# Prologue of a two-batch encoder layer: loads moved to a second queue, the first token tile done one weight tile at a time

## The chip, the cores and the metric

One NeuronCore of a Trainium2 chip runs the whole program. The metric is the device time of one execution in microseconds, the median of the runs shown. The engines are named as the profile names them: PE (TensorE), PEld (its weight loads), DVE (VectorE), ACT (ScalarE), POOL (GpSimd), SP (SyncE, which here only issues transfers).

## The reference, cut to what matters

One encoder layer with shared weights is applied to 512 sample tokens and 256 prompt tokens of width 1024, all float32:

```python
def _mixer(xn, w_in, ...):
    proj = xn @ w_in                       # (S, 1024) @ (1024, 4096)
    aq, ak, av, hq, hf_f, hf_b, hi, hg = jnp.split(proj, offs, axis=-1)
    ...
def _encode(x, norm_mix_pre, w_in, ...):
    mix = _mixer(_rmsnorm(x, norm_mix_pre[l]), w_in[l], ...)
    x = x + _rmsnorm(mix, norm_mix_post[l])
    ffn = _conv_ffn(_rmsnorm(x, norm_ffn_pre[l]), ...)
    x = x + _rmsnorm(ffn, norm_ffn_post[l])
```

The case is about the first step: the normalisation of x before the mixer, and the first block of columns of `xn @ w_in`, the 512 columns of `hi` (the values of the recurrent heads).

## The kernel before, in words

The 768 tokens are six tiles of 128 rows, x0 to x5. The weights come as a list of tiles of 1024 x 128 (512 KB each); the first four, W0 to W3, are the columns of `hi`, and W4 and on belong to the gates that follow. A weight tile lands in one of three RAW buffers (`raw`, line 209). `split` (line 231) turns it into a rounded high part (ACT, line 242) and a low part, tile minus high part (DVE, line 243), and then issues the load of the tile three further on (line 238), into the buffer that the DVE instruction has just read: that load waits on SP for that DVE instruction.

A token tile passes through `prenorm_rows` (line 307): half of its square sum on ACT (line 311), half on DVE (line 312), the mean (DVE, line 314), a power on POOL (line 304), then the scaling, two DVE instructions of 512 columns (line 317). `prenorm_transpose` (line 320) makes eight PE transposes into two PSUM banks, and `prenorm_evac` (line 326) splits them into a high part (two ACT copies, line 808) and a low part (two DVE subtractions, line 809).

`value_tile(n, i, ...)` (line 341) multiplies token tile i with weight tiles n and n+1: for each of eight k three products, high x high, low x high, high x low, 24 matmuls of 256 columns (line 346). The second of them already needs the low part of the tokens.

`run` (line 1099) writes this in program order: tile 0, W0, W1, tile 1, W2 and W3, then a loop over the tiles with `value_tile(0, i)`, transposes and evacuation of tile i+1, `prenorm_rows(i + 2)`, `value_tile(2, i)`. On SP and POOL the instructions stand in that program order (`manual_schedule`, line 1349). On PE, ACT and DVE the scheduler places them when the program is built, and each engine then runs its list in order.

`prologue_loads` (line 246) is a generator: its first part issues x0, the norm weights, the constants, W0, W1, x1, W2 and x2 on SP; its second part, after `split(4)`, x3 to x5 and the small parameters.

Of the kernel before, what the change touches and what calls it, by code (L numbers as in the profile page):

```python
# [10 lines left out]
OP = mybir.AluOpType  # L11

D = 1024
# [3 lines left out]
NTT = T // 128  # L17
# [79 lines left out]
class Encoder:  # L97
# [148 lines left out]
    def prologue_loads(self):  # L246
        nc, a = self.nc, self.a
        XT = self.S
        PR = self.PR = self.S + 9216
        self.WB1 = self.S + 8192  # L250

        def row(i):
            src = a["x_sample"][0, 128 * i:128 * i + 128, :] if i < 4 else \
                a["x_prompt"][0, 128 * (i - 4):128 * (i - 4) + 128, :]
            nc.sync.dma_start(self.v(XT + 1024 * i, 1024), src)

        row(0)
        nc.sync.dma_start(self.v(self.WB1, 1024), self.bcast("norm_mix_pre"))
        nc.sync.dma_start(self.cst, a["cst"])
        self.load(2)  # L260
        row(1)
        self.load(3)
        row(2)
        yield
        for i in range(3, NTT):
            row(i)
        nc.sync.dma_start(self.v(PR, 128, 0, 8), a["hgrn_lb_fwd"].rearrange("r (j p) -> (r j) p", p=128))
        nc.sync.dma_start(self.v(PR, 128, 8, 16), a["hgrn_lb_bwd"].rearrange("r (j p) -> (r j) p", p=128))
        o = ROWS["onorm"]
        for h in range(2):  # L270
            nc.sync.dma_start(self.v(PR + 64 * h, 64, o, o + 1), a["hgrn_out_norm"])
        o = ROWS["convb"]
        nc.sync.dma_start(self.v(PR, 128, o, o + NF), a["conv_b"].rearrange("l (k p) -> (l k) p", p=128))
        o = ROWS["convw"]
        nc.sync.dma_start(self.v(PR, 128, o, o + 3 * NF), a["conv_w"].rearrange("l w (k p) -> (l w k) p", p=128))
        nc.sync.dma_start(self.pm, a["pmask"].rearrange("p (l s) -> p l s", s=64))
        yield
# [27 lines left out]
        return r  # L305

    def prenorm_rows(self, i):
        nc = self.nc
        x, junk = self.S + 1024 * i, self.S + 7168
        sa, sb, ms = self.col(), self.col(), self.col()  # L310
        nc.scalar.activation(self.v(junk, 512), self.v(x, 512), AF.Square, accum_out=sa)
        nc.vector.tensor_tensor_reduce(self.v(junk + 512, 512), self.v(x + 512, 512), self.v(x + 512, 512), 1.0, D * EPS,
                                       op0=OP.mult, op1=OP.add, accum_out=sb)
        nc.vector.tensor_scalar(ms, sa, sb, 1.0 / D, op0=OP.add, op1=OP.mult)
        rs = self.rsqrt(ms)
        for c in (0, 512):
            nc.vector.scalar_tensor_tensor(self.v(x + c, 512), self.v(x + c, 512), rs, self.v(self.WB1 + c, 512),
                                           op0=OP.mult, op1=OP.mult)
# [780 lines left out]
    def run(self):  # L1099
        nc, ps = self.nc, self.ps  # L1100
# [6 lines left out]
        loads = self.prologue_loads()  # L1107
# [32 lines left out]
                due -= side()  # L1140


        self.prenorm_rows(0)
        self.prenorm_transpose(0)
        self.split(1)
        self.prenorm_evac(0)
        self.split(2)
        self.prenorm_rows(1)
        self.split(4)
        next(loads)  # L1150
        for i in range(5):
            self.value_tile(0, i, ps[:, i % 4, 0:256])
            self.prenorm_transpose(i + 1)
            self.prenorm_evac(i + 1)
            if i + 2 < NTT:
                self.prenorm_rows(i + 2)
            self.value_tile(2, i, ps[:, i % 4, 256:512])
            self.value_evac(self.V, i, ps[:, i % 4, :], 4)
# [22 lines left out]
        n = 4  # L1181
# [36 lines left out]
        order = (0, 2, 1, 3)  # L1218
# [105 lines left out]
        n = len(self.prods)  # L1324
# [46 lines left out]
```

## Time and profile before

| | |
|---|---|
| runs | 1001.67, 1003.06, 1003.91 us, median 1003.06 us |
| profiled execution, own time | 1004.14 us |
| its span in the trace | 1002.3 us |
| PE busy | 973.4 us (97%) |
| DVE, ACT, POOL busy | 727.2, 529.1, 53.4 us |
| mean granted clock | 0.997 |

The span runs from the first to the last instruction; the execution's own time is 1.8 us longer. PE is the busy engine of nearly every slice except the first: the page's forty slices of 25 us begin, for PE, with 5 tenths.

### The profile page before, as it was taken

To read this page: it belongs to the slowest core of one execution; us is meant where nothing else is said; L and a number is where in the kernel's file an instruction comes from. 1 tells how busy PE (TensorE), PEld (TensorE's weight loads), DVE (VectorE), ACT (ScalarE), POOL (GpSimd) and SP (SyncE) were. 2 spreads that over 40 slices of the span, in tenths; PEclk is the share of its full clock that TensorE was granted. 3 is DMA by queue.
4 is the path that set the end of the run, shared out by engine and by line. 5 is a ranking of instruction groups with operands and counts; after the bars stand their busy time and mean duration, and the time that the engine had idled before them with its cause. 6 is when DMAs were issued, how large, how long until landed. Compare 5 with 4: busy or idle time off the path is not lost.

```text
span 1002.3 us, 17989 instructions
## 1 busy us (share of the span) xinstructions
PE 973.4 (97%) x6988; PEld 867.0 (86%) x6988; DVE 727.2 (73%) x1324; ACT 529.1 (53%) x998; POOL 53.4 (5%) x45
## 2 busy tenths in 40 slices
PE   5999999999999999999989999999999999999997
PEld 5988888888988777678969999999999998888885
DVE  5435949495732775845799998878888879967966
ACT  4352626253233878844566555545555545665661
POOL 1100000000022101100110000000000000000002
PEclk9999999999999999999999999999999999999999
DMA  8132111111023221123434444534344449846643
GB/s 269 38 108 62 44 43 45 43 44 38 8 70 101 63 55 44 32 97 113 149 105 119 143 134 150 150 100 141 109 118 134 129 156 302 261 142 203 202 166 126
DMA packets 127655, 114.15 MB, mean 114 GB/s; under 512 B 6890, under 2 KB 113106, under 8 KB 127570
## 3 DMA queue, kind: packets, MB, share of 16 engines
q1 hardware_dynamic: 126706, 111.43, 36.3%
q10 hardware_dynamic: 864, 1.57, 0.4%
q8 instruction: 55, 0.90, 0.4%
q14 instruction: 30, 0.25, 0.1%
HBM read 89.18 MB, written 24.31 MB: 113 GB/s over the span
## 4 chain that ended last, share of the span: by engine, by line
PE 86%; DVE 6%; ACT 3%; DMA 2%; issue 2%; POOL 1%; SPq 0%; DVEq 0%; POOLq 0%; ACTq 0%
PE ps L850 29%; PE ps L338 21%; PE ps L1016 15%; PE ps L346 6%; PE ps L710 3%; PE ps L430 3%; PE ps L630 2%; PE ps L663 2%; PE ps L652 2%; PE ps L515 1%; PE ps L512 1%; DVE W L243 1%; DMA RAW<-w_in 1%; DVE S L645 1%; DVE V L747 1%
## 5 line engine op out<-in xcount | busy, mean ns | idle before, releaser
L338 PE MATMUL ps<-X,W 128*128 128x512 f32 (+1 forms) x1200 | 231.5, 343 | 0.0
L338 PEld LDWEIGHTS ps<-X,W 128*128 128x128 f32 x1200 | 185.6, 188 | 27.8 <-issue 2.4
L850 PE MATMUL ps<-XN,W 128*128 128x384 f32 x1056 | 189.4, 335 | 1.4 <-DVE W L243 0.5
L850 PEld LDWEIGHTS ps<-XN,W 128*128 128x128 f32 x1056 | 183.2, 188 | 3.2 <-DVE W L243 0.8
L1016 PE MATMUL ps<-W,XN 128*128 128x512 f32 x693 | 157.3, 389 | 0.0
L1016 PEld LDWEIGHTS ps<-W,XN 128*128 128x128 f32 x693 | 130.1, 188 | 27.0
L242 ACT ACTIVATE W<-RAW 128x512 fp32r<-128x512 f32 (+1 forms) x98 | 77.7, 796 | 137.0 <-PE ps L338 65.9
L850 PE MATMUL ps<-X,W 128*128 128x384 f32 x792 | 144.3, 339 | 3.1 <-ACT X L799 1.7
L850 PEld LDWEIGHTS ps<-X,W 128*128 128x128 f32 x792 | 139.5, 188 | 4.5 <-ACT X L799 2.4
L243 DVE TENSOR_TENSOR W<-RAW,W 128x512 fp32r<-128x512 f32 (+1 forms) x88 | 75.1, 855 | 41.0 <-ACT W L242 41.0
L242 ACT ACTIVATE W<-V 128x512 fp32r<-128x512 f32 x99 | 61.9, 629 | 61.3 <-PE ps L850 47.8
L346 PE MATMUL ps<-W,X 128*128 128x256 f32 (+1 forms) x432 | 66.7, 311 | 3.7 <-ACT X L808 2.7
L243 DVE TENSOR_TENSOR W<-V,W 128x512 fp32r<-128x512 f32 x99 | 66.8, 684 | 2.7 <-ACT W L242 2.7
L346 PEld LDWEIGHTS ps<-W,X 128*128 128x128 f32 x432 | 61.2, 194 | 5.7 <-ACT X L808 3.3
L710 PE MATMUL ps<-W,X 128*128 128x512 f32 (+1 forms) x288 | 57.2, 344 | 0.0
L710 PEld LDWEIGHTS ps<-W,X 128*128 128x128 f32 x288 | 44.0, 189 | 7.0 <-issue 1.6
L304 POOL TENSOR_TENSOR sm<-sm 128x1 f32<-128x1 f32 x24 | 18.5, 780 | 586.1 <-DVE sm L1030 479.4
L242 ACT ACTIVATE XN<-X 128x384 fp32r<-128x384 f32 x77 | 39.2, 517 | 12.5 <-DMA X<-sd 7.2
L243 DVE TENSOR_TENSOR XN<-X,XN 128x384 fp32r<-128x384 f32 x77 | 41.6, 548 | 3.2 <-ACT XN L242 3.2
L242 ACT ACTIVATE W<-EX 128x512 fp32r<-128x512 f32 x39 | 24.6, 630 | 32.3 <-PE ps L850 17.5
L397 ACT ACTIVATE S<-S 128x384 f32<-128x384 f32 x28 | 15.1, 538 | 39.9 <-PE ps L430 39.2
L243 DVE TENSOR_TENSOR W<-EX,W 128x512 fp32r<-128x512 f32 x39 | 26.7, 684 | 12.2 <-ACT W L242 12.2
(214 smaller groups left out, 1289.0 us busy)
## 6 DMA issues: line engine op xcount, KB each, us to landing
RAW<-w_in SPq DMA_DIRECT2D x32, 512.0 KB
X<-sd SPq DMA_DIRECT2D x44, 192.0 KB
RAW<-w_gate SPq DMA_DIRECT2D x14, 512.0 KB
RAW<-w_up SPq DMA_DIRECT2D x13, 512.0 KB
RAW<-w_down SPq DMA_DIRECT2D x26, 256.0 KB
X<-gd SPq DMA_DIRECT2D x33, 192.0 KB
EX<-w_up SPq DMA_DIRECT2D x9, 512.0 KB
EX<-w_down SPq DMA_DIRECT2D x18, 256.0 KB
```

The costliest lines, as they stand in the source:

```text
L242: nc.scalar.activation(self.r(hi, n), self.v(src, n), AF.Copy)
L243: (eng or nc.vector).tensor_tensor(self.r(lo, n), self.v(src, n), self.v(hi, n), op=OP.subtract)
L304: self.nc.gpsimd.tensor_tensor(r, mean, self.mhalf, op=OP.pow)
L338: nc.tensor.matmul(out, self.r(wo + 128 * k, 128), self.r(xo + T * k + t0, tn), start=(k == 0 and first), stop=(k == NK - 1 and last))
L346: self.nc.tensor.matmul(out, self.r(xo + T * k + 128 * i, 128), self.rap(wo + 128 * k, [[1024, tiles], [1, 128]]), start=(k == 0 and first ...
L430: nc.tensor.matmul(ps[64 * cb:64 * cb + 64, b + h, 64 * c:64 * c + 64], self.v(kt + t0, 64, *HALF[h]), qv(t0, h), start=True, stop=True)
L630: nc.tensor.matmul(ps[:, 4 + h, 0:L], self.r(QS + T * h + t0 + 128 * i, 128), self.r(x + T * h + t0, L), start=z, stop=not z)
L652: nc.tensor.transpose(ps[:, 6 + h, 128 * kt:128 * kt + 128], ms(j, n, h)[:, 128 * kt:128 * kt + 128], self.ident)
L663: nc.tensor.matmul(o[64 * h:64 * h + 64], self.v(vb + 128 * kt + 64 * h, 64), self.v(pt(s, h) + L * kt, L), start=kt == 0, stop=kt == L // ...
L710: nc.tensor.matmul(out, self.r(mo + T * f + 128 * i, 128), rhs, start=(f == 0 and first), stop=(f == NK - 1 and last))
L850: nc.tensor.matmul(out, self.r(wo + 128 * k, 128), self.r(xo + H * k, H), start=kind in BEGINS and k == 0 and first, stop=k == 3 and last, ...
L1016: nc.tensor.matmul(self.down_bank(k, i), self.r(go + 128 * i, 128), self.r(wo, 512), start=f == 0 and k in ("P1", "P5", "P2") and first, s ...
```

## The change: what it does

- SP's first part ends with W0. W1, x1 and W2 are issued by ACT, behind its square sum of x0. x2 is no longer in the first part: it goes with x3 to x5 in the last part, which SP reaches behind W6.
- `prenorm_rows` is cut in two, `prenorm_sums` and `prenorm_scale`, so that the loads of ACT can stand between them for tile 0.
- From the sums of tile 0 to the split of W1, ACT and DVE also keep the program order.
- `value_tile(0, 0)` becomes two: W0 alone, then W1 alone, 24 matmuls of 128 columns each.

```diff
-        def row(i):
+        def row(i, eng=nc.sync):
...
-            nc.sync.dma_start(self.v(XT + 1024 * i, 1024), src)
+            eng.dma_start(self.v(XT + 1024 * i, 1024), src)
...
         nc.sync.dma_start(self.cst, a["cst"])
-        self.load(2)
-        row(1)
-        self.load(3)
-        row(2)
+        self.load(1)
         yield
-        for i in range(3, NTT):
+
+        self.load(2, nc.scalar)
+        row(1, nc.scalar)
+        self.load(3, nc.scalar)
+        yield
+        for i in range(2, NTT):
             row(i)
...
-        self.prenorm_rows(0)
+        order = self.tc.manual_schedule(engines={mybir.EngineType.Activation, mybir.EngineType.DVE})
+        order.__enter__()
+        self.prenorm_sums(0)
+        next(loads)
+        self.prenorm_scale(0)
         self.prenorm_transpose(0)
         self.split(1)
         self.prenorm_evac(0)
         self.split(2)
+        order.__exit__(None, None, None)
         self.prenorm_rows(1)
         self.split(4)
         next(loads)
         for i in range(5):
-            self.value_tile(0, i, ps[:, i % 4, 0:256])
+            if i == 0:
+
+                for n in range(2):
+                    self.value_tile(n, 0, ps[:, 0, 128 * n:128 * n + 128], 1)
+            else:
+                self.value_tile(0, i, ps[:, i % 4, 0:256])
```

What stands in a row where, first on SP from the constants on. RAW is a weight tile, S from x_sample a token tile. Before:

```order
L259 DMA cst<-cst 128x130
L228 DMA RAW<-w_in 128x8x128 x2
L255 DMA S<-x_sample 128x1024
L228 DMA RAW<-w_in 128x8x128
L255 DMA S<-x_sample 128x1024
L228 DMA RAW<-w_in 128x8x128 x4
L255 DMA S<-x_sample 128x1024
L255 DMA S<-x_prompt 128x1024 x2
```

and with the change:

```order
L259 DMA cst<-cst 128x130
L228 DMA RAW<-w_in 128x8x128 x5
L255 DMA S<-x_sample 128x1024 x2
L255 DMA S<-x_prompt 128x1024 x2
```

The five weight loads are now W0 and W3 to W6 (W1 and W2, and x1 between them, are ACT's), and x2 stands behind all of them, where it stood ahead of W3.

On DVE, from the scaling of tile 0 (line 317 before, 327 now) to the scaling of tile 1. Line 312, now 318, is a square sum; 243 a weight tile's low part; 809, now 819, a token tile's low part; 314, now 320, the mean. Before:

```order
L317 SCALAR_TENSOR_TENSOR S<-S,sm 128x512 x2
L243 TENSOR_TENSOR W<-RAW,W 128x1024 x2
L809 TENSOR_TENSOR X<-ps,X 128x4x128 x2
L312 ISA S,sm<-S 128x512
L312 ISA sm 128x1
L314 TENSOR_SCALAR sm<-sm 128x1
L243 TENSOR_TENSOR W<-RAW,W 128x1024
L317 SCALAR_TENSOR_TENSOR S<-S,sm 128x512 x2
```

and with the change:

```order
L327 SCALAR_TENSOR_TENSOR S<-S,sm 128x512 x2
L318 ISA S,sm<-S 128x512
L318 ISA sm 128x1
L243 TENSOR_TENSOR W<-RAW,W 128x1024
L819 TENSOR_TENSOR X<-ps,X 128x4x128 x2
L243 TENSOR_TENSOR W<-RAW,W 128x1024
L320 TENSOR_SCALAR sm<-sm 128x1
L243 TENSOR_TENSOR W<-RAW,W 128x1024
L327 SCALAR_TENSOR_TENSOR S<-S,sm 128x512 x2
```

The square sum of x1 moved up from behind the first two weight tiles and the low part of tile 0 to a place ahead of them all.

On DVE again, directly behind that, from the low part of W3 to the scaling of tile 2. Before:

```order
L312 ISA S,sm<-S 128x512
L312 ISA sm 128x1
L243 TENSOR_TENSOR W<-RAW,W 128x1024
L809 TENSOR_TENSOR X<-ps,X 128x4x128 x2
L314 TENSOR_SCALAR sm<-sm 128x1
L317 SCALAR_TENSOR_TENSOR S<-S,sm 128x512 x2
```

and with the change:

```order
L243 TENSOR_TENSOR W<-RAW,W 128x1024
L318 ISA S,sm<-S 128x512
L318 ISA sm 128x1
L320 TENSOR_SCALAR sm<-sm 128x1
L327 SCALAR_TENSOR_TENSOR S<-S,sm 128x512
L819 TENSOR_TENSOR X<-ps,X 128x4x128 x2
L327 SCALAR_TENSOR_TENSOR S<-S,sm 128x512
```

The low part of tile 1 stood behind the square sum of x2; now it stands behind its mean and the first half of its scaling too. The low part of tile 2 likewise moved behind the scalings of x3 and x4.

## Rows read from the trace of the kernel before

**Rows 1.** The page: span, and busy time of each engine.

```profile
span 1002.3 us, 17989 instructions
PE 973.4 (97%) x6988; PEld 867.0 (86%) x6988; DVE 727.2 (73%) x1324; ACT 529.1 (53%) x998; POOL 53.4 (5%) x45
```

**Rows 2.** PE by stretches: window, length, busy (count), granted clock, DMA share, GB/s.

```profile
0.00:19.58 19.58, 8.57 (x44) 1.00 0.92 271
19.58:54.69 35.11, 35.11 (x295) 1.00 0.20 69
54.69:1002.30 947.61, 929.67 (x6651) 1.00 0.37 112
```

**Rows 3.** PE's waits, longest first, first and last of fourteen: total us, times, longest.

```profile
PE ps L323 <- DVE S L317: 7.3, 1, 7.3
...
PE ps L346 <- DVE W L243: 0.2, 1, 0.2
```

**Rows 4.** Chain that ended last, in order of time: start us, us, what.

```profile
19.58 5.61 PE ps L346 x45
25.18 0.87 PE ps L323 x8
26.05 5.70 PE ps L346 x48
...
32.62 5.92 PE ps L346 x48
```

**Rows 5.** DVE's timeline, 0 to 32 us: start us, us, what [idle before <-releaser].

```profile
6.48 1.41 DVE L317 SCALAR_TENSOR_TENSOR S<-S,sm 128x512 f32<-128x512 f32 x2 [0.93 <-DMA S<-norm_mix_pre]
...
12.57 1.28 DVE L809 TENSOR_TENSOR X<-ps,X 128x512 fp32r<-128x512 f32 x2
...
14.57 0.21 DVE L314 TENSOR_SCALAR sm<-sm 128x1 f32<-128x1 f32 x1
...
16.36 1.41 DVE L317 SCALAR_TENSOR_TENSOR S<-S,sm 128x512 f32<-128x512 f32 x2 [0.45 <-POOL sm L304]
...
18.30 1.22 DVE L243 TENSOR_TENSOR W<-RAW,W 128x1024 fp32r<-128x1024 f32 x1
...
25.00 0.69 DVE L312 CUSTOM_DVE_ANT_0 S<-S 128x512 f32<-128x512 f32 x1 [2.08 <-DMA S<-x_sample]
...
27.37 1.28 DVE L809 TENSOR_TENSOR X<-ps,X 128x512 fp32r<-128x512 f32 x2
```

**Rows 6.** ACT's timeline, what ended its waits for loads.

```profile
8.57 1.06 ACT L242 ACTIVATE W<-RAW 128x1024 fp32r<-128x1024 f32 x1 [3.33 <-DMA RAW<-w_in]
10.34 1.06 ACT L242 ACTIVATE W<-RAW 128x1024 fp32r<-128x1024 f32 x1 [0.72 <-DMA RAW<-w_in]
...
13.44 1.06 ACT L242 ACTIVATE W<-RAW 128x1024 fp32r<-128x1024 f32 x1 [0.46 <-DMA RAW<-w_in]
14.80 0.63 ACT L311 ACTIVATE S<-S 128x512 f32<-128x512 f32 x1 [0.30 <-DMA S<-x_sample]
...
58.26 1.06 ACT L242 ACTIVATE W<-RAW 128x1024 fp32r<-128x1024 f32 x1 [2.11 <-DMA RAW<-w_in]
```

**Rows 7.** SP's queue: when a load is issued, and how long the issue took.

```profile
3.73 3.03 SPq L255 DMA_DIRECT2D S<-x_sample  x1
...
19.55 0.37 SPq L228 DMA_DIRECT2D RAW<-w_in  x1
19.97 0.57 SPq L255 DMA_DIRECT2D S<-x_sample  x1
...
54.10 1.51 SPq L228 DMA_DIRECT2D RAW<-w_in  x2
```

**Rows 8.** PE's timeline: the first products.

```profile
13.31 4.52 PE L346 MATMUL ps<-W,X 128*128 128x256 f32 x23 [0.79 <-DVE X L809]
```

**Rows 9.** All engines, one stretch: PE, PEld, DVE, ACT, POOL, clock, DMA share, GB/s.

```profile
9.30:11.90 2.60, 0.00 (x0) 0.00 (x0) 1.69 (x2) 1.88 (x4) 0.00 (x0) 1.00 1.09 346
```

**Rows 10.** The chain again, later: matmuls of 128 columns that stand alone.

```profile
127.06 0.42 PE ps L515 x2
```

More of the change, by code (lines that the diff above doesn't have):

```diff
@@ L307, in prenorm_rows, with prenorm_sums @@
     def prenorm_rows(self, i):
+        self.prenorm_sums(i)
+        self.prenorm_scale(i)
+    def prenorm_sums(self, i):
         nc = self.nc
         x, junk = self.S + 1024 * i, self.S + 7168
-        sa, sb, ms = self.col(), self.col(), self.col()
+        sa, sb, self.ms1 = self.col(), self.col(), self.col()
         nc.scalar.activation(self.v(junk, 512), self.v(x, 512), AF.Square, accum_out=sa)
@@ L313, in prenorm_rows, with prenorm_scale @@
                                        op0=OP.mult, op1=OP.add, accum_out=sb)
-        nc.vector.tensor_scalar(ms, sa, sb, 1.0 / D, op0=OP.add, op1=OP.mult)
-        rs = self.rsqrt(ms)
+        nc.vector.tensor_scalar(self.ms1, sa, sb, 1.0 / D, op0=OP.add, op1=OP.mult)
+    def prenorm_scale(self, i):
+        nc = self.nc
+        x = self.S + 1024 * i
+        rs = self.rsqrt(self.ms1)
         for c in (0, 512):
```

## The prediction

> **What bounds the kernel now.** I read the page first: PE is busy for 973.4 us of a span of 1002.3 us [rows 1]. So a change of the prologue can only win PE's idle time there, or add to it. Then PE by stretches [rows 2]: up to 19.58 us PE works 8.57 us and stands 11.0; from 19.58 to 54.69 it has no idle time at all; and in the other 948 us it stands 18 us. Third, PE's waits [rows 3]: all fourteen are for DVE or ACT, none names a transfer. What PE does after 19.58 us therefore starts a fixed work later than 19.58, and the prologue counts one for one in the end: a delay at tile 1 or 2 is a delay of the whole program.
>
> The chain in order of time gives the marks that I measure against [rows 4]. 45 of the 48 products of `value_tile(2, 0)` and `value_tile(0, 1)` run from 19.58 to 25.18, then the transposes of x2 (0.87 us), then 48 products from 26.05 in 5.70 us, that is 0.119 us each. 24 of them take 2.85 us, so `value_tile(0, 1)` begins at 25.18 - 2.85 = 22.3 us and `value_tile(0, 2)` at 26.05 + 2.85 = 28.9 us.
>
> Two more views tell what feeds PE. DVE's timeline [rows 5] has the price of each instruction: a square sum 0.69, a weight tile's low part 1.22, both halves of a token tile's low part 1.28, the mean 0.21, both halves of a scaling 1.41. ACT's and SP's rows [rows 6, 7] tell when transfers land: W0 8.57, W1 10.34, W2 13.44, x2 14.80 us. In these microseconds the DMA engines are full (share 1.09, 346 GB/s [rows 9]).
>
> **The change part by part.** *DVE stands for x1 first.* The square sum of x1 now stands ahead of W0's low part. Call x1's landing a. The bytes come in the same order as before (x0, norm weights, constants, W0, W1, x1, W2) through engines that were full, so a lies between W1's 10.34 and W2's 13.44 [rows 6]; both ends are possible, I take the middle, 11.9. From there DVE does, in its new order, the sum 0.69, W0 1.22, low part of tile 0 1.28, W1 1.22, mean 0.21, W2 1.22, scaling of x1 1.41, W3 1.22: 8.47 us, so W3 is done at 20.4. W3's load itself is issued behind W0's low part, 11.9 + 1.91 = 13.8. A weight tile that met an empty queue was issued at 54.10 and landed at 58.26, 4.16 us [rows 6, 7]; by that W3 lands at 18.0 and its copy on ACT ends at 19.0, when DVE is just done with the scaling of x1 (19.2): it hides.
>
> *x2 comes late.* Before, x2 had landed at 14.80. Now it stands on SP behind W6, and W6 waits for W3's low part: 20.4. In the trace of before the next tile, x3, was in this very place: W6 issued at 19.55, x3 at 19.97, x3 there at 25.00, 5.45 us after W6's issue [rows 5, 7]. So x2 lands at 20.4 + 5.45 = 25.9. Call it b. The lower bound is one tile's 4.16, b = 24.6.
> The Trainium skill's page "DMA: Bandwidth & Descriptors" (Anatomy of one DMA — SWDGE (gpsimd) path) puts a transfer at some 2.0 us fixed and its bytes at 436 GB/s. By that W6 and x2 would need an estimated 4.4 us and the forecast would be 1.0 us lower; but that page's price of one weight tile, 3.2 us, is contradicted by the 4.16 us of the trace, and it is measured on another path.
>
> *What waits for x2.* The low part of tile 1 now stands behind the mean and the first scaling of x2, and `value_tile(0, 1)` needs it in its second product. The same chain is in the trace for x3: sum at 25.00, low part at 27.37 [rows 5], its first half (0.64) done at 28.0, 3.0 us behind the landing. So `value_tile(0, 1)` starts at 25.9 + 3.0 = 28.9, where before it was 22.3: 6.6 us lost.
>
> *PE's own work up to there hides.* Low part of tile 0 is half done at 11.9 + 0.69 + 1.22 + 0.64 = 14.5, and PE begins then (13.31 before). 48 products of 128 columns take the place of 24 of 256. Their price is not in the trace: transposes of the same size run at 0.87 / 8 = 0.109 us [rows 4], full matmuls of that size took 0.42 / 2 = 0.21 us [rows 10]. I take 0.109, as these are as densely packed as the transposes. The first 23 products of before took 4.52 us, 0.196 each [rows 8], though the granted clock reads 1.00 (the upper level, 2.4 GHz) throughout [rows 2]; I add these 23 x 0.077 = 1.8 us. So the 48 end at 14.5 + 5.2 + 1.8 = 21.5, transposes of x1 22.4, `value_tile(2, 0)` 25.2: PE then stands 3.7 us until 28.9. At 0.21 each it ends at 30.0, only 1.1 later than 28.9, and the next wait takes most of that up. The dearer form therefore costs almost nothing as long as x2 is late, and 2 to 7 us if it weren't.
>
> *The next tile.* Low part of tile 2 stands behind the scalings of x3 and x4. Counted from b: 2.37 to the low part of tile 1, 1.28 for it, then half a scaling 0.71, sum 0.69, mean 0.21, sum 0.69, scaling 1.41, mean 0.21, sum 0.69, scaling 1.41, half a low part 0.64: 10.3 us, 36.2; with up to two waits for POOL of 0.45 [rows 5] 37.1; I take 36.5. PE would be there at 28.9 + 2.85 + 0.87 + 2.85 = 35.5, so this one binds: 36.5 against 28.9 is 7.6 us lost. From there x5 is the last thing on DVE and PE sets the pace; the 48 products from 32.62 had 0.2 us of such a wait themselves (5.92 against 5.70 [rows 4]), which goes. Net **7.4 us lost**.
>
> *Nothing else counts.* ACT's three issues cost some 0.4 us each where it stood 3.33 us before W0 [rows 6]; even if one blocks for 3.03, as x1's did on SP [rows 7], DVE stands until 11.9 and covers it. The held order by itself costs nothing beyond these places; behind the prologue the lists of all engines are the same.
>
> The sum: the profiled execution took 1004.14 us, its span and 1.8 around it, so its like would be 1011.5; it lay 1.1 above the median of the runs, 1003.06, to which I hold the forecast: **1010.5 us**.
>
> **The rivals.** *x2 is quick enough.* If x2 landed at 22.2, 3.0 ahead of PE's 25.2, PE would set the pace and only the later start and the 48 slim products would show: 25.2 - 22.3 = 2.9 us, 1006.0. Against it: that is 1.8 us behind its issue, and the shortest row is 4.16. Chance 0.03.
>
> *Not slower: two queues bring the loads side by side.* If ACT's loads did not queue behind SP's, x1 could be there when the scaling of tile 0 ends, 6.48 + 1.41 = 7.9 us [rows 5]. Then DVE is not held up, PE begins 7.9 + 2.6 = 10.5 (the sum, W0 and half a low part) instead of 13.31, and if x2 is also ready, `value_tile(0, 1)` starts when PE is ready for it: 10.5 + 7.0 + 0.87 + 2.85 = 21.2 against 22.3, 1.1 us won (1002.0), and 2.9 (1000.2) if the slow first products don't recur. It decides at x2: it must land by 18.2, 7 us before I have it. For it: transfers share nothing but the DMA engines. Against it: these were full at 346 GB/s [rows 9], and x2 is issued behind W3's work, wherever x1 came from. The Trainium skill's page "DMA: Bandwidth & Descriptors" (Issuing engines are not separate DMA queues) says that issuing from several engines saves only the issue time, since all run on the same 16 DMA engines; the trace's full share agrees. Chance 0.05.
>
> *The delay is swallowed, the change does nothing in the end.* Some later wait could have its own timing, so that 7 us less of PE time ahead of it don't show: 1003.1. Against it: PE's 18 us of later waits are all for DVE or ACT [rows 2, 3], which themselves follow PE's results. Chance 0.04.
>
> **How the numbers follow.** The forecast has 0.88. Its own bounds: a from 10.34 to 13.44 moves all by -1.6 to +1.5; x2 at the one-tile price -1.3; slow products again after PE's stand of 3.7 us cost 24 x 0.077 = 1.8, of which 1.0 is covered by the wait for tile 2, so +0.8: 1007.6 to 1012.8. With the first rival's 1006.0 and rounding up, 1006.0 to 1013.0; outside are the two rivals that aren't slower, 0.09, and what I have not seen. 0.2% is 2 us, about what a measurement of this kernel can tell from no change. Faster by more than that: the better end of the second rival, 0.03. Within: the rest of it and the third, 0.06. Slower: the forecast and the first rival, 0.91.
>
> **What would show it.** In the profile of the changed kernel: DVE's square sum of x1 begins near 11.9 us with a wait for its load, ahead of W0's low part; SP's issue of x2 stands behind W6 at 20 to 21 us; DVE waits for x2 until 25 to 26 us; PE has an idle time of 2 to 5 us before a product of line 356, released by DVE's line 819, ending near 29 us, and a second of about 1 us near 36. I am wrong if PE is without idle time from about 20 us on, if x2 lands before 22 us, or if the gap is there and the time behind it doesn't move.

## The result, and the profile after

The changed kernel takes 1015.65 us (median of 1014.29 to 1016.34) against 1003.06: a ratio of 1.012, 95% interval 1.0102 to 1.0137. It is slower, as forecast, but by 12.6 us where 7.4 were forecast, and the time lies above the range's 1013.0. The profiled execution took 1015.65 us itself, 1.75 more than its span. Its page:

```profile
span 1013.9 us, 18036 instructions
PE 981.5 (97%) x7012; PEld 874.8 (86%) x7012; DVE 727.5 (72%) x1324; ACT 528.3 (52%) x998; POOL 53.7 (5%) x45
```

To see where the 11.6 us of span came from I use one mark throughout: the moment at which the chain of waits first reaches the next products, those of line 338 (348 now) with the weights of the gates. Before it is 54.69 us, the end of the second stretch of [rows 2]; now it is 64.40, **9.71 us later**. Two rows of the chain, in order of time (start, length, what):

```profile
38.68 3.00 PE ps L356 x23
...
64.40 5.61 PE ps L348 x32
```

PE by stretches up to the first narrow products, to the mark, and to the end (window, length, busy (count), weight loads, DVE, ACT, POOL, clock, DMA share, GB/s):

```profile
0.00:14.66 14.66, 2.45 (x10) 1.86 (x10) 4.89 (x11) 6.80 (x10) 0.76 (x5) 1.00 0.69 219
14.66:64.40 49.74, 48.77 (x353) 48.56 (x354) 23.83 (x47) 14.47 (x29) 5.32 (x6) 1.00 0.28 91
64.40:1013.90 949.50, 930.25 (x6651) 824.40 (x6650) 698.74 (x1268) 507.08 (x961) 47.65 (x34) 1.00 0.37 112
```

Against [rows 2]: up to the mark PE was busy for 8.57 + 35.11 = 43.7 us and is now busy for 51.2, 7.5 more; its idle time went from 11.0 to 13.2, 2.2 more. I had forecast the opposite, that the loss would be idle time. Behind the mark 949.50 us stand against 947.61, 1.9 more. PE's timeline shows the busy time (start, length, what, in brackets the idle time ahead of it and its releaser):

```profile
14.66 10.29 PE L356 MATMUL ps<-W,X 128*128 128x128 f32 x47 [4.59 <-DVE X L819]
24.74 1.93 PE L333 MATMUL ps<-cst,S 128*128 128x128 f32 x8
26.32 7.52 PE L356 MATMUL ps<-W,X 128*128 128x256 f32 x48
33.68 1.04 PE L333 MATMUL ps<-cst,S 128*128 128x128 f32 x8
...
38.68 3.00 PE L356 MATMUL ps<-W,X 128*128 128x256 f32 x23 [0.97 <-DVE X L819]
```

The 47 narrow products take 0.219 us each, twice the 0.109 I had chosen; the transposes behind them take 1.93 us where the next eight take 1.04; and the 48 products of 256 columns begin at the same pace, 7.52 us in all. PE has no idle time from 14.66 to 37.7 us. The idle time before tile 1, 3.7 us in the forecast, isn't there. That is the first sign that the prediction named for its being wrong.

The other half came as forecast. DVE's timeline:

```profile
12.16 0.69 DVE L318 CUSTOM_DVE_ANT_0 S<-S 128x512 f32<-128x512 f32 x1 [4.58 <-DMA S<-x_sample]
...
13.92 1.28 DVE L819 TENSOR_TENSOR X<-ps,X 128x512 fp32r<-128x512 f32 x2
...
27.76 0.69 DVE L318 CUSTOM_DVE_ANT_0 S<-S 128x512 f32<-128x512 f32 x1 [7.17 <-DMA S<-x_sample]
...
30.12 1.28 DVE L819 TENSOR_TENSOR X<-ps,X 128x512 fp32r<-128x512 f32 x2
...
37.94 1.28 DVE L819 TENSOR_TENSOR X<-ps,X 128x512 fp32r<-128x512 f32 x2
```

DVE stands for x1 until 12.16 (forecast 11.9), ahead of W0's low part; x2 lands at 27.76 (25.9), the low part of tile 1 stands behind its first scaling, at 30.12 (28.3), and the low part of tile 2 holds PE up at 38.68 (36.5). So two chains reach tile 1 at the same time: x2's lets its second product start at 30.8 us (30.12 and half of 1.28), and PE's own work ends at about 31. At tile 2 it is x2's chain that PE still waits for, 0.97 us. What each of them would cost alone, these traces can't say. The experiments take them apart.

Why x2 landed 1.9 us later than forecast can be read here. All engines by single microseconds, columns as in [rows 9] (the last two are the DMA share and GB/s), before:

```profile
13.00:14.00 1.00, 0.69 (x3) 0.69 (x4) 1.00 (x3) 0.56 (x1) 0.00 (x0) 1.00 1.00 354
14.00:15.00 1.00, 1.00 (x7) 1.00 (x7) 0.89 (x4) 0.70 (x2) 0.14 (x1) 1.00 1.15 306
...
20.00:21.00 1.00, 1.00 (x11) 1.00 (x10) 0.84 (x3) 0.00 (x0) 0.08 (x1) 1.00 0.18 47
```

and after:

```profile
13.00:14.00 1.00, 0.00 (x0) 0.00 (x0) 1.00 (x2) 0.32 (x1) 0.00 (x0) 1.00 0.01 3
14.00:15.00 1.00, 0.34 (x2) 0.35 (x2) 1.00 (x3) 0.73 (x1) 0.00 (x0) 1.00 0.00 0
...
20.00:21.00 1.00, 1.00 (x7) 1.00 (x6) 0.58 (x1) 0.00 (x0) 0.00 (x0) 1.00 0.96 275
```

and, from the chain of the changed kernel, W6's issue on SP and the load of x2 behind it:

```profile
20.61 0.37 SPq L228
...
21.03 6.71 DMA S<-x_sample
```

While DVE stands for x1 no RAW buffer comes free and SP issues nothing: the DMA engines, full before (shares 1.00 and 1.15), do nothing from 13 to 15 us. W3, W4 and W5 are then issued between 14.0 and 17.6 us, and when W6 is issued the engines are still busy (share 0.96), where they were nearly empty before (0.18). x2 landed 7.15 us behind W6's issue, not 5.45. That the one follows from the other is read from the traces and not tested by itself, but the other runs point the same way: without the empty stretch x2 landed 5.62 us (old_x2_late) and 5.92 us (held_late) behind W6's issue, with it 6.32 (changed_busy) and 6.68 (wide). So the size of this delay varies by 0.8 us among runs that have it.

### The profile page after: what moved, and what is told of

Its sections match the earlier page's. It is cut to its first block, busy times and chain, and to the rows that moved or that the text cites. A ratio compares the mean times of both kernels' runs of the same rounds, so it can differ in the third digit from the quotient of the medians.

```text
span 1013.9 us, 18036 instructions
## 1 busy us (share of the span) xinstructions
PE 981.5 (97%) x7012; PEld 874.8 (86%) x7012; DVE 727.5 (72%) x1324; ACT 528.3 (52%) x998; POOL 53.7 (5%) x45
## 4 chain that ended last, share of the span: by engine, by line
PE 84%; DVE 6%; DMA 3%; ACT 2%; issue 2%; POOL 1%; SPq 1%; DVEq 0%; POOLq 0%; ACTq 0%
PE ps L860 27%; PE ps L348 21%; PE ps L1026 15%; PE ps L356 5%; PE ps L720 4%; PE ps L440 3%; PE ps L640 2%; PE ps L673 2%; PE ps L662 2%; PE ps L525 1%; DMA S<-x_sample 1%; PE ps L522 1%; DMA RAW<-w_in 1%; POOL sm L306 1%; DVE S L655 1%
## 5 line engine op out<-in xcount | busy, mean ns | idle before, releaser
L356 PE MATMUL ps<-W,X 128*128 128x256 f32 (+2 forms) x456 | 73.5, 322 | 6.2 <-DVE X L819 5.6
L356 PEld LDWEIGHTS ps<-W,X 128*128 128x128 f32 x456 | 68.6, 209 | 7.7 <-DVE X L819 6.0
L720 PEld LDWEIGHTS ps<-W,X 128*128 128x128 f32 x288 | 44.0, 188 | 7.0 <-issue 1.6
```

What stands on the lines that cost most here:

```text
L356: self.nc.tensor.matmul(out, self.r(xo + T * k + 128 * i, 128), self.rap(wo + 128 * k, [[1024, tiles], [1, 128]]), start=(k == 0 and first ...
L720: nc.tensor.matmul(out, self.r(mo + T * f + 128 * i, 128), rhs, start=(f == 0 and first), stop=(f == NK - 1 and last))
```

## The experiments

The profiles' marks, with what they are later than 54.69, and the ratios of time to the kernel before on the same chip. "Narrow" are products of 128 columns for tile 0 (for tile 4 in old_slim4).

| run | narrow | x2 | mark | ratio, 95% |
|---|---|---|---|---|
| after | yes | late | 64.40, +9.71 | 1.012, 1.0102 to 1.0137 |
| wide | no | late | 57.39, +2.70 | 1.0029, 1.0019 to 1.004 |
| x2_early | yes | early | 63.38, +8.69 | 1.0097, 1.0082 to 1.0112 |
| x2_early_wide | no | early | 56.81, +2.12 | 1.0027, 1.0015 to 1.0038 |
| old_slim0 | yes | early | 61.73, +7.04 | 1.0095, 1.008 to 1.011 |
| old_x2_late | no | late | 55.02, +0.33 | 1.0004, 0.9995 to 1.0014 |
| old_slim4 | tile 4 | early | 57.05, +2.36 | 1.0054, 1.0039 to 1.0069 |
| changed_busy | yes | late | 63.80, +9.11 | 1.011, 1.0096 to 1.0124 |
| held_slim | yes | early | 58.56, +3.87 | 1.0048, 1.0031 to 1.0064 |
| held_slim_busy | yes | early | 54.32, -0.37 | 1.0004, 0.9993 to 1.0015 |
| held_wide | no | early | 54.12, -0.57 | 0.9989, 0.9979 to 0.9998 |
| held_late | no | late | 61.65, +6.96 | 1.0063, 1.005 to 1.0077 |
| held_pool | no | early | 54.44, -0.25 | 1.0005, 0.9995 to 1.0014 |

**One part of the change taken back.** First the narrow products (wide):

```diff
-            if i == 0:
-                for n in range(2):
-                    self.value_tile(n, 0, ps[:, 0, 128 * n:128 * n + 128], 1)
-            else:
-                self.value_tile(0, i, ps[:, i % 4, 0:256])
+            self.value_tile(0, i, ps[:, i % 4, 0:256])
```

> The changed kernel with its first token tile computed by 24 products of 256 columns again; loads and held order as changed. This also lets the low part of tile 1 move ahead of the square sum of x2 on DVE. Theory L (the late load of x2 sets the time): x2 still lands near 27.8 us, its transposes start near 30 instead of 25.2 us, so some 5 us are left of the 12.6: about 1008. Rival P (PE's slow products of 128 columns set the time): with them gone PE is on time again but for a start 1.3 us later: 1004 to 1005.

1006.76 us against 1003.98: 7.0 of the 9.71 us at the mark are gone with the narrow products, though x2 is still late. But the edit moved something else too, which DVE's timeline shows:

```profile
21.34 1.29 DVE L819 TENSOR_TENSOR X<-ps,X 128x512 fp32r<-128x512 f32 x2 [1.59 <-ACT X L818]
26.46 0.69 DVE L318 CUSTOM_DVE_ANT_0 S<-S 128x512 f32<-128x512 f32 x1 [3.83 <-DMA S<-x_sample]
```

The scheduler now puts the low part of tile 1 (21.34) ahead of x2's sum, so PE has tile 1 to work on while it waits. So this run doesn't say that a late x2 costs nothing; it says that the order in which it would cost is there only with the narrow products.

Then the late x2 (x2_early, and both together, x2_early_wide):

```diff
         self.load(3, nc.scalar)
+        row(2, nc.scalar)
         yield
-        for i in range(2, NTT):
+        for i in range(3, NTT):
```

> The changed kernel with x2 issued by ACT behind W2, so that it lands near 15 to 16 us; the products of 128 columns stay. On DVE the low part of tile 1 now stands behind the first scaling of x3, which is loaded behind W6. Theory L in its plain form (x2 alone): most is regained, 1004 to 1005. Theory L with the order (whatever tile is loaded behind W6 holds up the low part of tile 1): x3 lands near 26, 1009 to 1011. Rival P: PE has no idle time from 14.7 us on in the changed kernel and is as late without x2's wait, first product of tile 1 near 31 us: 1011 to 1013.

> Both of these together: x2 issued by ACT behind W2, and 256 columns again. Left of the change are ACT's issues and the square sum of x1 ahead of the low part of W0. L and P both: 1 to 2 us above the kernel before, 1004 to 1005; anything more would be a third cause (the loads on ACT, the held order).

x2_early gives back only 1.0 us at the mark. Its narrow products take 10.29 us again and its transposes 1.93. But it doesn't rid the chain of a late load: x3, which now comes first behind W6, lands at 27.15 us, where x2 had landed at 27.76, and the low part of tile 1 stands behind its first scaling. DVE's timeline, then PE's:

```profile
27.15 0.69 DVE L319 CUSTOM_DVE_ANT_0 S<-S 128x512 f32<-128x512 f32 x1 [3.38 <-DMA S<-x_sample]
...
30.25 2.99 PE L357 MATMUL ps<-W,X 128*128 128x256 f32 x23 [0.27 <-DVE X L820]
...
37.70 2.99 PE L357 MATMUL ps<-W,X 128*128 128x256 f32 x23 [0.62 <-DVE X L820]
```

PE waits for that chain only 0.27 and 0.62 us. Without these two waits an estimated 8.69 - 0.27 - 0.62 = 7.8 us would be left, and they would be PE's own pace and its later start. x2_early_wide keeps 2.1 us: what remains of the change there is the loads on ACT and the order that puts x1's sum ahead of W0, and PE's main row of first products begins at 15.37 us, where it was 13.31 [rows 8].

**One part alone, in the kernel before.** old_slim0 has the narrow products of tile 0, old_slim4 has them for tile 4 instead, long after PE's last idle time (first piece; old_slim0 has `i == 0`), old_x2_late moves x2 behind W6 (second piece):

```diff
-            self.value_tile(0, i, ps[:, i % 4, 0:256])
+            if i == 4:
+                for n in range(2):
+                    self.value_tile(n, 4, ps[:, 0, 128 * n:128 * n + 128], 1)
+            else:
+                self.value_tile(0, i, ps[:, i % 4, 0:256])
...
-        row(2)
         yield
-        for i in range(3, NTT):
+        for i in range(2, NTT):
```

> The kernel before, with only the first token tile's products as 48 of 128 columns; all loads as before. On DVE the low part of tile 1 then stands behind the first scaling of x3 (landing at 25.0 before). Theory L plain: nothing is late but PE's own 2 to 4 us, 1005 to 1007. Theory L with the order: the low part of tile 1 waits for x3, 25.0 + 3.0 = 28 us, against 22.3: 1008 to 1009. Rival P: products from 13.3 us at 0.219 us, 23.8, slow transposes 25.5, slow products 30: 7 to 8 us lost, 1010 to 1011.

> The kernel before, with only x2's load moved behind W6, still issued by SP; 256 columns. On DVE the low part of tile 1 stands ahead of the square sum of x2 here. W6 is issued near 19 us as W3 lands sooner, x2 lands near 24.5 to 25, its transposes start near 27 to 27.5 instead of 25.2. Theory L: 2 to 3 us lost, 1005 to 1006. Rival P: nothing lost, 1003.

> The kernel before, with only tile 4's products with W0 and W1 as 48 of 128 columns, in the middle of a dense stretch of PE; the order on DVE, ACT and SP is that of before. If the form itself costs 0.21 us (rival P, form): these 48 take 10 us in place of 2.85, 1010. If it costs as much as a transpose, 0.11 us, at full rate: 5.2 us, 1005.5. If many such products make PE slow by themselves (rival P, rate): they start at 0.11 and end near 0.21 us, and the transposes and products behind them are slow too: 1006 to 1012.

The narrow products alone cost 9.7 us (1013.3 against 1003.59), of which 7.04 lie ahead of the mark. From 13.23 us up to there PE works without a stand, so nothing that is late plays a part in these 7.04. The late x2 alone costs 0.2, not to be told from nothing; but there, as in wide, DVE makes the low part of tile 1 (19.26 us) ahead of x2's sum, so this run too lacks the order in which x2 holds up tile 1. The same 48 products at tile 4 are much cheaper. PE's timeline of old_slim0:

```profile
13.23 10.29 PE L346 MATMUL ps<-W,X 128*128 128x128 f32 x47 [0.90 <-DVE X L809]
23.32 1.93 PE L323 MATMUL ps<-cst,S 128*128 128x128 f32 x8
24.90 7.55 PE L346 MATMUL ps<-W,X 128*128 128x256 f32 x48
```

and the chain of old_slim4, where 48 narrow products and 24 of 256 columns follow each other:

```profile
38.43 0.87 PE ps L323 x8
39.30 8.19 PE ps L346 x72
```

8.19 less the 2.85 us of 24 wide ones leaves 5.34, 0.111 us each: that is the price that I had taken. So the form costs 48 x 0.111 - 2.85 = 2.5 us where PE is at its upper level, and the mark moves by 2.36. At tile 0 it costs 7.0. What differs is not the form but the place.

**Is it the rate of an engine that has stood?** Two runs give PE work to do while DVE makes the low part of tile 0: matmuls of 512 columns, whose results nobody reads, in front of the narrow ones. changed_busy does it in the changed kernel (eight). The others need a kernel whose x2 is early: held_slim holds program order on ACT and DVE through the first loop and loads x2 behind W3, held_slim_busy adds twelve such matmuls to it, and held_wide is held_slim with 256 columns. First the added work, then what makes held_slim of the changed kernel:

```diff
         self.split(1)
+        for _ in range(8):
+            nc.tensor.matmul(ps[:, 3, :], self.r(self.hi(0), 128), self.r(self.hi(0), 512), start=True, stop=True)
         self.prenorm_evac(0)
...
         yield
-        for i in range(2, NTT):
+        row(2)
+        yield
+        for i in range(3, NTT):
...
         self.split(1)
+        next(loads)
         self.prenorm_evac(0)
         self.split(2)
-        order.__exit__(None, None, None)
-        self.prenorm_rows(1)
+        self.prenorm_sums(1)
+        self.split(3)
+        self.prenorm_scale(1)
...
             self.value_evac(self.V, i, ps[:, i % 4, :], 4)
+        order.__exit__(None, None, None)
```

> The changed kernel with the program order held on ACT and DVE through the whole loop of the prologue, x1's square sum behind the low part of W1, and x2 loaded behind W3; products of 128 columns. No low part stands behind a later tile's load any more. Theory L: everything is regained and the earlier start shows, 1001 to 1003. Rival P: PE starts near 11 us, 48 slow products to 21.3, slow transposes and products to 28 against 22.3: 1007 to 1009.

> The same with 256 columns again. L and P both: no late load, no slow products; PE starts its products near 13 us as W1 sets that, W3's low part near 18.6 us instead of 19.5: 0 to 1.5 us better than the kernel before, 1001.5 to 1003.

> The kernel held_slim (program order held on ACT and DVE through the first loop, x2 loaded behind W3, narrow products of 128 columns for tile 0) with twelve more matmuls of 512 columns, results unused, between the first transposes and the first products. It is added work. x2 is early here, so only the rate is left. Theory A (the rate follows what PE did before): narrow products at some 0.111 us each, transposes of tile 1 at some 0.13 each, the weights-stationary products at 53.5 to 55.5 us instead of 58.56, time 1002 to 1004.5. Theory B (the form is dear in this place): 47 narrow products in some 10.3 us again, 58.5 us or later, time 1008 or more.

held_slim against held_slim_busy settles it. PE's timeline of the first:

```profile
11.09 10.29 PE L358 MATMUL ps<-W,X 128*128 128x128 f32 x47 [0.90 <-DVE X L821]
21.17 1.93 PE L335 MATMUL ps<-cst,S 128*128 128x128 f32 x8
22.75 6.47 PE L358 MATMUL ps<-W,X 128*128 128x256 f32 x48
```

and of the second:

```profile
9.27 3.85 PE L1164 MATMUL ps<-W 128*128 128x512 f32 x12 [0.26 <-ACT W L242]
12.96 5.47 PE L358 MATMUL ps<-W,X 128*128 128x128 f32 x48
18.27 1.06 PE L335 MATMUL ps<-cst,S 128*128 128x128 f32 x8
19.09 5.94 PE L358 MATMUL ps<-W,X 128*128 128x256 f32 x48
```

The narrow products start 1.9 us later and end 2.9 us earlier; the 4.24 us at the mark, and 1.0048 to 1.0004 in the ratio, come from added work. The loads don't explain it: from 10 to 20 us the DMA engines move 283 GB/s in the first and 274 in the second. The cost is PE's rate, and the rate depends on what PE did before, not on the instructions. The Trainium skill's page "TensorE: Matmul & The Clock Gate" (Part 1: The HAM clock gate) says that the lower clock is the default and that activity releases it; these two rows agree.

> The changed kernel with eight more matmuls of 512 columns on PE, put between the first transposes and the first products, on a PSUM bank that nobody reads; they multiply the high part of W0 with itself and their result is left unused, so it is added work that keeps PE occupied while DVE makes the low part of tile 0. Theory A (the slow rate of 0.219 us for each of the 47 narrow products belongs to an engine that stood still before them): the narrow products fall to some 0.111 us each, PE reaches the second token tile by 22 to 24 us and then stands for the load of x2 until about 30.8 us; since x2's chain alone allows that tile no sooner, the start of the weights-stationary products moves from 64.4 us only to 61 to 63, and the time to 1012 to 1014. Theory B (the narrow form costs 0.219 here whatever went before): no idle time on PE, 64 us and 1015 to 1016. Theory C (the narrow products alone make the loss, x2 none): 57 us and 1005 to 1008.

This run shows the clock itself. PE alone in its stretches (window, length, busy (count), granted clock, DMA share, GB/s):

```profile
13.07:14.85 1.78, 0.00 (x0) 1.00 0.01 3
14.85:17.00 2.15, 2.15 (x19) 1.00 0.61 167
17.00:23.02 6.02, 6.02 (x31) 0.50 0.81 229
23.02:24.60 1.58, 1.58 (x10) 0.50 1.12 335
24.60:27.00 2.40, 2.40 (x13) 0.50 1.01 378
27.00:28.80 1.80, 1.80 (x16) 0.94 1.03 407
```

PE still stood for 1.78 us behind the added matmuls. Then the clock was up, and 19 narrow products ran in 2.15 us, 0.113 each. At 17.0 us, in the midst of them, the granted clock fell to 0.50, 1.2 GHz, and the other 28 took the 6.02 us up to the transposes, 0.215 each. It came back between 27.0 and 28.8, among products of 256 columns. The changed kernel's 0.219 us are thus those of the lower level, though its rows read 1.00 there (14.66 to 64.40 above). So the run shows both rates in one row of equal products, but doesn't rid the prologue of the lower one. It gives a clean answer on x2. PE's timeline:

```profile
24.60 4.38 PE L356 MATMUL ps<-W,X 128*128 128x256 f32 x25
30.24 2.99 PE L356 MATMUL ps<-W,X 128*128 128x256 f32 x23 [1.26 <-DVE X L819]
```

PE is 1.26 us early now and waits for the low part of tile 1. x2's sum began at 27.13 us, 0.63 before that of the changed kernel, and the mark is 0.60 earlier: from x2 to the mark both take 36.7 us. So with part of PE's time given back x2's chain alone holds nearly all of the 9.7 us.

**The forecast's mechanism alone.** held_late is held_wide with x2 behind W6 again (`row(2)` in the last part) and the evacuation of tile 1, its high part on ACT and its low part on DVE, behind x2's sums and scaling, in products of 256 columns:

```diff
-            self.prenorm_evac(i + 1)
+            if i:
+                self.prenorm_evac(i + 1)
             if i + 2 < NTT:
                 self.prenorm_rows(i + 2)
+            if not i:
+                self.prenorm_evac(1)
```

> The kernel held_wide (program order held through the first loop, 256 columns for tile 0) with x2 loaded behind W6 again and the low part of tile 1 put behind the scaling of x2 on DVE: the mechanism of the forecast alone, without narrow products. Theory D (a late x2 with the low part of tile 1 behind it costs by itself what was forecast): x2 lands at 24.5 to 26 us, the products of tile 1 begin near 28.5 to 29.5 us where they began near 22, the weights-stationary products start at 59 to 61 us instead of 54.12, time 1008 to 1010. Rival (the narrow products alone cost time): 54 to 55.5 us, 1003 to 1004.

1009.66 us, and 7.53 us at the mark against held_wide. PE alone, from the end of the products that it had:

```profile
22.00:25.90 3.90, 0.05 (x1) 0.90 1.03 401
25.95:29.00 3.05, 2.45 (x10) 0.50 0.70 246
29.00:31.00 2.00, 2.00 (x10) 0.50 0.08 21
31.00:33.00 2.00, 2.00 (x16) 0.77 0.00 0
```

PE stands 3.90 us, within the 2 to 5 that the prediction named, and after that runs at 0.50 until almost 32 us: 10 products in 2.00 us, 0.2 each with 256 columns. PE's timeline and the chain behind it:

```profile
25.95 0.58 PE L356 MATMUL ps<-W,X 128*128 128x256 f32 x1 [3.90 <-ACT X L818]
...
27.14 1.97 PE ps L333 x8
29.10 9.85 PE ps L356 x71
```

PE waits here for ACT's high part, since that stands behind x2's square sum too, and once more for 0.60 us ahead of the transposes. So 4.5 of the 7.53 us are standing. The other 3.0 are the lower clock: 1.97 us for the transposes (0.87 in [rows 4]), 9.85 for 71 products (8.4 at 0.119 each), and 0.58 for the first one. A late x2 that holds up tile 1 thus makes PE stand as the forecast says. That the sum agrees as well, 7.53 against 7.4, is partly luck: the forecast had no lower clock behind the stand in its sum, only 0.8 us of it in its range, and instead a second wait at tile 2, which doesn't occur here.

**A better version.** held_wide is 1002.77 against 1003.59; its interval ends at 0.9998, so it may be ahead of the kernel before by about 1 us, hardly more than can be measured. held_pool moves the low part of W2 from DVE to GpSimd and the scaling of x1 ahead of it:

```diff
-                          self.nc.gpsimd if 26 <= n < 36 else self.nc.vector)
+                          self.nc.gpsimd if n == 2 or 26 <= n < 36 else self.nc.vector)
...
-        self.prenorm_sums(1)
-        self.split(3)
-        self.prenorm_scale(1)
+        self.prenorm_rows(1)
```

> The kernel held_wide with the low part of W2 made by GpSimd instead of DVE and the scaling of x1 ahead of the split of W2, a candidate for a better version than both kernels. If DVE's list sets PE's pace in the first 20 us, PE's short waits for low parts go and the weights-stationary products start 0.5 to 1.5 us sooner than 54.12, time 1001 to 1002.5. If PE's own work sets it, nothing changes: 54.1 us, 1002.5 to 1003. If GpSimd is too slow for a tile that is needed this early, 55 us or later and 1003.5 or more.

No gain: 54.44 against 54.12. DVE's scaling of x1 got slower instead, 3.51 us for its two halves where [rows 5] has 1.41:

```profile
14.65 3.51 DVE L329 SCALAR_TENSOR_TENSOR S<-S,sm 128x512 f32<-128x512 f32 x2 [0.67 <-POOL sm L308]
```

while GpSimd works on W2's low part from 14.58 to 16.95 us: the first half takes most of it and ends only behind GpSimd's work. Nothing is left of the time that DVE was to save.

## Why the prediction was right in sign and wrong in size

- *DVE stands for x1 first*: right. 12.16 against 11.9; PE's first row of products begins at 14.66 against 14.5. x2_early_wide prices the order and the loads on ACT at 2.1 us.
- *x2 comes late*: right in mechanism, mis-sized. W6 was issued at 20.61 (20.4), but x2 landed 7.15 us later, not 5.45. I took the delay of x3 from a trace in which the DMA engines had run empty before W6 (share 0.18); in the changed kernel the stand of DVE for x1, which I had priced only for PE, empties them at 13 to 15 us and has them full at 20 (0.96). With the 0.2 of the later issue that is 1.9 us, and as x2's chain leads to 38.68 it counts in full. The range let x2 land earlier behind W6 (1.3 us) and never later.
- *What waits for x2*, *The next tile*: right. From x2's sum to the two low parts 2.36 and 10.18 us; I had 2.37 and, to half of the second one, 10.6 (measured 10.9).
- *PE's own work up to there hides*: **this step failed.** "I take 0.109" and 1.8 us for a slow start should have been 0.219 for 47 products and the lower level for the transposes and a good part of the next products too. PE's idle time of 3.7 us was never there; what happened is nearer to the aside "At 0.21 each it ends at 30.0" (measured: about 31), which the sum didn't follow. I had seen 0.196 in [rows 8] beside a clock that reads 1.00 and took it for something that 23 products end by themselves; with products of 128 columns it lasted until the products of 256 columns. That the sign held is no merit of this step: by old_slim0 it costs 7.0 us at the mark with no late x2 at all, the upper end of the "2 to 7 us if it weren't", and "almost nothing as long as x2 is late" holds only because two delays, of 9.1 us (changed_busy) and some 7.8 (x2_early less its waits), lie side by side instead of adding up. As a plan it misleads: whoever brings x2 early, as the forecast would suggest, gains 1.0, since x3 is late in its place and PE is no sooner there.
- *Nothing else counts*: not quite. Behind the mark the changed kernel took 1.9 us more. Of PE's waits there, those that differ are in the stage of line 850 (860 now): 0.29, 0.61 and 0.86 us against 0.25 and 0.31. Over all fourteen profiles that rest lies between 945.7 and 951.1 us, in the seven with narrow products 1.8 us higher on average; the two that differ only in added matmuls (held_slim, held_slim_busy) differ by 4.0. That difference is one of executions, not of kernels: the profiled ones are held_slim's longest (1009.95, median 1008.07) and held_slim_busy's shortest (1001.79, median 1003.81), and the medians differ by 4.26 us, as the marks do. A single profile can thus be off by 2 us there, and the cause of the 1.9 stays open.
- The sum: 9.71 - 7.4 = 2.3 us at the mark (1.9 from x2's landing, the rest in steps of a few tenths), 1.9 behind it, and 1.1 because I held the forecast to the median while this profiled execution is the median itself: 5.3, against the 5.15 by which the forecast missed. So the failed step above was wrong in mechanism, but PE's slower pace lies hidden beside x2's chain and didn't put the time outside the range (in changed_busy, with part of it given back, the mark moves only as far as x2's landing does). What put it there, together, are x2's landing, forecast 1.9 us too early, the 1.9 behind the mark, taken as nothing, and the 1.1.

Of the rivals, a quick x2 was priced at 1006.0; x2_early shows 1013.48: its price too stood on 0.109, and it left out that x3 would then be the late tile. The side-by-side queues and the swallowed delay didn't occur.

## What to carry to other kernels

Before you split a product into narrower ones, price it at both levels of PE's clock: 0.111 and 0.219 us here, while a product of twice the width cost 0.119 and 0.2. Close to PE's idle time the lower one counts, and work put into the gap can be worth more than an earlier start. When a term is hidden by another wait, test it with that wait taken out: here either of two delays alone made most of the loss (7.0 us in old_slim0, 7.5 in held_late, of 9.7), and giving back part of one while the other stood gained next to nothing (0.6 us in changed_busy, as much as x2 landed earlier there). And an engine that waits in program order for a late load also holds back the buffers, and so the transfers, behind it.

## What the runs showed of the hardware that was not expected

- The granted clock in the rows reads 1.00 in the first 17 us of every kernel here, also where products take twice their later time; only after a fall (changed_busy at 17.0, held_late while PE stands up to 25.95 us) do rows read 0.50 beside the same durations. The durations decide. The Trainium skill's page "TensorE: Matmul & The Clock Gate" (Part 1: The HAM clock gate) warns that the trace events of the clock on trn2 have been seen to be unreliable; these rows agree.
- The clock can fall while PE is busy: in changed_busy it fell 2.15 us into a dense row of narrow products, after a stand of 1.78 us. In held_slim_busy, without that stand, the same products left it up.
- Twelve matmuls whose results nobody reads (3.85 us) made held_slim's prologue 4.2 us shorter. That brings it level with the kernel before (ratio 1.0004), not ahead of it.
